# A prefix log-sum-exp scan: seven of eight batches in a hardware loop, four tile buffers instead of five

## The chip, the cores and the metric

One core of a Trainium2 chip. The metric is the device time of one execution in microseconds (us). The kernel before: 1257.1 us, median of 3 runs (1256.9 to 1266.4). All runs used below were classed as fast.

## The reference

```python
B, S, D = 8, 4096, 2048
x = np.random.randn(B, S, D).astype(np.float32)

out[:, 0, :] = x[:, 0, :]
for t in range(1, S):
    mx = np.maximum(out[:, t-1, :], x[:, t, :])
    out[:, t, :] = mx + np.log(np.exp(out[:, t-1, :] - mx) + np.exp(x[:, t, :] - mx))
```

It is a running log-sum-exp along S. Batches are independent of each other. 268 MB are read and 268 MB written, so the kernel has 537 MB to move.

## The kernel before

A batch is cut into 8 tiles of 512 rows (128 partitions x 4 rows), each 4 MB, and each tile into 4 column pieces of 512. For a piece, ScalarE takes Exp, TensorE sums down the 128 partitions with a triangular matrix, VectorE adds up the 4 rows of each partition, and ScalarE takes Ln and writes the result over the input in the same tile buffer. SyncE (SP) issues the loads, ScalarE's queue (ACTq) the stores. All 64 tiles are unrolled in the program.

```python
iopool = ctx.enter_context(tc.tile_pool(name="iopool", bufs=5))      # tile buffers
...
x_v = x.rearrange("b (k p r) d -> b k p r d", p=P, r=R)
o_v = out.rearrange("b (k p r) d -> b k p r d", p=P, r=R)
tiles = [(b, k) for b in range(B) for k in range(NBLK)]              # 8 x 8
pieces = [(b, k, c) for b, k in tiles for c in range(NC)]            # x 4

def load(b, k):
    t = iopool.tile([P, R, D], f32, name=f"io_{b}_{k}", tag="io")
    io[b, k] = t
    nc.sync.dma_start(out=t, in_=x_v[b, k])                          # L72
...
def front(b, k, c):                                                  # load, Exp, matmuls, adds
    if c == 0:
        load(b, k)
    ...
    nc.scalar.activation(et, t[:, :, cols(c)], ACT.Exp)              # L84
    ...
def back(b, k, c):
    t = io[b, k]
    nc.scalar.activation(t[:, :, cols(c)], sums.pop((b, k, c)), ACT.Ln)   # L106
    if (b, k) == tiles[-1]:
        ...                                                          # the very last tile goes out in 3 pieces
    elif c == NC - 1:
        nc.scalar.dma_start(out=o_v[b, k], in_=t)                    # L113

for n, piece in enumerate(pieces):
    front(*piece)
    if n >= 1:
        carry(*pieces[n - 1])
    if n >= LAG:                                                     # LAG = 2
        back(*pieces[n - LAG])
for piece in pieces[-LAG:]:
    back(*piece)
```

A buffer is free again when its store has landed; only then may the next load into it be issued.

The softmax here doesn't subtract the row's maximum and nothing guards it: scores larger than these inputs give would overflow.

Of the kernel before, what the change touches and what calls it, by code (L numbers as in the profile page):

```python
# [1 line left out]

# [4 lines left out]


@with_exitstack
def kernel(  # L10
    ctx: ExitStack,
    tc: tile.TileContext,
    x: bass.AP,
    out: bass.AP,
):









    nc = tc.nc
    f32 = mybir.dt.float32
    bf16 = mybir.dt.bfloat16
    ACT = mybir.ActivationFunctionType
    nc.scalar.preload_act_table_set("natural_log_exp_and_others")  # L29

    B, S, D = x.shape
    P = 128
    R = 4
    NBLK = S // (P * R)
    FD = 512
    NC = D // FD
    LAG = 2

    const = ctx.enter_context(tc.tile_pool(name="const", bufs=1))
    Li = const.tile([P, P], bf16)  # L40
    masks.make_upper_triangular(nc, Li, val=1.0, diag=True)
    Ls = const.tile([P, P], bf16)
    masks.make_upper_triangular(nc, Ls, val=1.0, diag=False)

    last = const.tile([P, P], f32)
    nc.gpsimd.memset(last, 1.0)  # L46
    nc.gpsimd.affine_select(  # L47
        out=last, in_=last, compare_op=mybir.AluOpType.is_ge, fill=0.0,
        base=-(P - 1), pattern=[[0, P]], channel_multiplier=1,
    )  # L50

    iopool = ctx.enter_context(tc.tile_pool(name="iopool", bufs=5))
    epool = ctx.enter_context(tc.tile_pool(name="epool", bufs=4))
    spool = ctx.enter_context(tc.tile_pool(name="spool", bufs=3))
    ppool = ctx.enter_context(tc.tile_pool(name="ppool", bufs=2, space=bass.MemoryType.PSUM))

    x_v = x.rearrange("b (k p r) d -> b k p r d", p=P, r=R)
    o_v = out.rearrange("b (k p r) d -> b k p r d", p=P, r=R)

    tiles = [(b, k) for b in range(B) for k in range(NBLK)]  # L60
    pieces = [(b, k, c) for b, k in tiles for c in range(NC)]
    io = {}
    sums = {}
    banks = {}

    def cols(c):
        return slice(c * FD, (c + 1) * FD)

    def load(b, k):
        t = iopool.tile([P, R, D], f32, name=f"io_{b}_{k}", tag="io")  # L70
        io[b, k] = t
        nc.sync.dma_start(out=t, in_=x_v[b, k])  # L72

    def bank(b, k, c):
        if (b, k, c) not in banks:
            banks[b, k, c] = ppool.tile([P, FD], f32, name=f"ps_{b}_{k}_{c}", tag=f"ps{c}")
        return banks[b, k, c]

    def front(b, k, c):
        if c == 0:  # L80
            load(b, k)
        t = io[b, k]
        et = epool.tile([P, R, FD], bf16, name="et")
        nc.scalar.activation(et, t[:, :, cols(c)], ACT.Exp)  # L84
        ps = bank(b, k, c)
        for r in range(R):
            nc.tensor.matmul(  # L87
                ps, Li if r == 0 else Ls, et[:, r, :],
                start=(k == 0 and r == 0), stop=(r == R - 1), skip_group_check=True,
            )  # L90
        st = spool.tile([P, R, FD], f32, name="st")
        nc.vector.tensor_copy(st[:, 0, :], ps)  # L92
        for r in range(1, R):
            nc.vector.tensor_add(st[:, r, :], st[:, r - 1, :], et[:, r, :])  # L94
        sums[b, k, c] = st

    def carry(b, k, c):
        if k < NBLK - 1:
            nc.tensor.matmul(  # L99
                bank(b, k + 1, c), last, sums[b, k, c][:, R - 1, :],  # L100
                start=True, stop=False, skip_group_check=True,
            )

    def back(b, k, c):
        t = io[b, k]
        nc.scalar.activation(t[:, :, cols(c)], sums.pop((b, k, c)), ACT.Ln)  # L106
        if (b, k) == tiles[-1]:

            if c > 0:
                part = slice(0 if c == 1 else c * FD, (c + 1) * FD)  # L110
                nc.scalar.dma_start(out=o_v[b, k][:, :, part], in_=t[:, :, part])
        elif c == NC - 1:
            nc.scalar.dma_start(out=o_v[b, k], in_=t)  # L113

    for n, piece in enumerate(pieces):
        front(*piece)
        if n >= 1:
            carry(*pieces[n - 1])
        if n >= LAG:
            back(*pieces[n - LAG])  # L120
    for piece in pieces[-LAG:]:
        back(*piece)


# [1 line left out]
_INS = ['x']  # L126
_OUTS = [((8, 4096, 2048), 'float32')]


# [23 lines left out]
```

## Time and profile before

| | |
|---|---|
| time, median | 1257.1 us |
| DMA rate in the steady part | 431 to 435 GB/s |
| DMA time of a tile, 4 MB in and 4 MB out | 19.4 us |
| ScalarE work of a tile, 8 x 1.9 us | 15.2 us |
| load, issue to landing | 31.4 us |
| store, issue to landing | 38.5 us |

From the page of the kernel before: the span, the busy time of the engines, and the two rows of DMA in 40 equal slices of the span (busy share in tenths, then GB/s).

```profile
span 1255.4 us, 5457 instructions
...
PE 636.7 (51%) x1443; PEld 216.8 (17%) x1472; DVE 703.3 (56%) x1024; ACT 930.0 (74%) x513; POOL 1.5 (0%) x10
...
DMA  9999999999999999999999999999999999999997
GB/s 401 429 430 431 435 429 433 434 433 434 434 432 433 434 432 432 433 431 432 431 431 433 434 432 434 433 434 435 431 434 431 432 432 433 432 431 431 434 428 285
```

The DMA row is full but for the last slice; no compute engine is above 74%. The Trainium skill, "DMA: Bandwidth & Descriptors", section "Where 436 GB/s comes from", gives 435 GB/s as the ceiling of the fabric (beside about 358 as HBM's share for one core, which this trace passes with one core at work), and this trace agrees: 431 to 435. Both queues always hold work, as the times to landing in the list of DMA issues show (KB of one transfer, then median us): one transfer would need about 9.7 us alone (an estimate: 4.19 MB at 432 GB/s), and takes 31 to 39 since others share the engines with it.

```profile
io<-in_x_dram SPq DMA_DIRECT2D x64, 4096.0 KB, 31.4
out_dram<-io ACTq DMA_DIRECT2D x63, 4096.0 KB, 38.5
```

The two groups of ScalarE (count, busy us, mean ns | idle us before them, and what ended most of it) and ScalarE's timeline over two tiles (start us, duration us, what, idle before and what ended it):

```profile
L84 ACT ACTIVATE et<-io 128x2048 bf16<-128x2048 f32 x256 | 485.2, 1897 | 305.8 <-DMA io<-in_x_dram 305.8
...
L106 ACT ACTIVATE io<-st 128x2048 f32<-128x2048 f32 x256 | 484.6, 1894 | 4.6 <-DVE st L94 4.5
```

```profile
615.87 1.91 ACT L84 ACTIVATE et<-io 128x2048 bf16<-128x2048 f32 x1 [4.87 <-DMA io<-in_x_dram]
...
623.21 0.34 ACTq L113 DMA_DIRECT2D out_dram<-io  x1
...
635.21 1.91 ACT L84 ACTIVATE et<-io 128x2048 bf16<-128x2048 f32 x1 [4.83 <-DMA io<-in_x_dram]
...
642.55 0.34 ACTq L113 DMA_DIRECT2D out_dram<-io  x1
```

ScalarE idles almost for one thing alone, the arrival of a load (305.8 us before Exp, L84). Its stores (L113) leave every 19.4 us, as soon as the tile's last Ln is done.

### The profile page before, as it was taken

Reading aid. Unit: us, or ns where it says so; the run is one execution under the profiler, and the core shown is the slowest. Engines: PE = TensorE matmul, PEld = TensorE weight load, DVE = VectorE, ACT = ScalarE, POOL = GpSimd, SP = SyncE. Lnnn points to the kernel's source line nnn. Section 1 sums busy time; section 2 is a strip of 40 time slices with the busy share of each in tenths; the row PEclk is TensorE's granted clock in tenths of the full one; section 3 lists DMA queues with packets and bytes.
Section 4 is the critical chain, followed back from the end, with each engine's and each line's share of the span. In section 5 each row is a group of like instructions: output and inputs, shape, how many; then the busy total and the mean of one; then the engine's idle time right before and its main releaser. Section 6 shows DMA issues by size and latency. Waiting matters only on the chain.

```text
span 1255.4 us, 5457 instructions
## 1 busy us (share of the span) xinstructions
PE 636.7 (51%) x1443; PEld 216.8 (17%) x1472; DVE 703.3 (56%) x1024; ACT 930.0 (74%) x513; POOL 1.5 (0%) x10
## 2 busy tenths in 40 slices
PE   3655445554455455554546544455455454555532
PEld 1211112111111111111111111111111121111210
DVE  3675556555565655655555556465565555655553
ACT  5987768677686786876867768677686776867865
POOL 0000000000000000000000000000000000000000
PEclk9898688785887857878577886887767878678785
DMA  9999999999999999999999999999999999999997
GB/s 401 429 430 431 435 429 433 434 433 434 434 432 433 434 432 432 433 431 432 431 431 433 434 432 434 433 434 435 431 434 431 432 432 433 432 431 431 434 428 285
DMA packets 19903, 537.22 MB, mean 428 GB/s; under 512 B 2080, under 2 KB 2080, under 8 KB 3616
## 3 DMA queue, kind: packets, MB, share of 16 engines
q1 hardware_dynamic: 9216, 268.44, 49.7%
q10 hardware_dynamic: 10656, 268.44, 49.7%
q8 instruction: 11, 0.18, 0.1%
q14 instruction: 20, 0.16, 0.0%
HBM read 268.44 MB, written 268.44 MB: 428 GB/s over the span
## 4 chain that ended last, share of the span: by engine, by line
DMA 69%; ACT 14%; DVE 5%; PE 5%; issue 5%; ACTq 0%; another core or an unknown queue 0%; DVEq 0%; SPq 0%
DMA io<-in_x_dram 67%; ACT io L106 9%; ACT et L84 5%; DVE st L94 4%; PE ps L87 3%; DMA out_dram<-io 2%; PE ps L99 2%; DVE st L92 1%; ACTq L106 0%; DVEq L94 0%; ACTq L113 0%; ACTq L84 0%; DVEq L92 0%; SPq L72 0%
## 5 line engine op out<-in xcount | busy, mean ns | idle before, releaser
L84 ACT ACTIVATE et<-io 128x2048 bf16<-128x2048 f32 x256 | 485.2, 1897 | 305.8 <-DMA io<-in_x_dram 305.8
L94 DVE TENSOR_TENSOR st<-st,et 128x512 f32<-128x512 f32 x768 | 531.0, 692 | 43.4
L106 ACT ACTIVATE io<-st 128x2048 f32<-128x2048 f32 x256 | 484.6, 1894 | 4.6 <-DVE st L94 4.5
L92 DVE COPY st<-ps 128x512 f32<-128x512 f32 x256 | 176.7, 690 | 492.5 <-PE ps L87 468.4
L99 PE MATMUL ps<-st,last 128*128 128x512 f32 x448 | 306.3, 772 | 137.6 <-DVE st L94 135.8
L87 PE MATMUL ps<-et,Li 128*128 128x512 bf16 x256 | 125.3, 489 | 459.9 <-ACT et L84 458.2
L87 PE MATMUL ps<-et,Ls 128*128 128x512 bf16 x739 | 280.5, 500 | 1.6 <-issue 1.1
L87 PEld LDWEIGHTS <-Ls 128*128 128x128 bf16 x768 | 89.5, 116 | 691.2 <-issue 662.0
L99 PEld LDWEIGHTS ps<-st,last 128*128 128x128 f32 x448 | 96.6, 238 | 249.3 <-DVE st L94 226.0
L87 PEld LDWEIGHTS <-Li 128*128 128x128 bf16 x256 | 30.7, 120 | 78.0 <-issue 70.5
L29 ACT ACT_TABLE_LOAD x1 | 1.3, 1283 | 0.8 <-PEq L137 0.8
masks.py:66 POOL TENSOR_SCALAR_AFFINE_SELECT Ls<-Ls 128x128 bf16<-128x128 bf16 x1 | 0.3, 297 | 0.0
masks.py:66 POOL TENSOR_SCALAR_AFFINE_SELECT Li<-Li 128x128 bf16<-128x128 bf16 x1 | 0.3, 296 | 0.0
L47 POOL TENSOR_SCALAR_AFFINE_SELECT last<-last 128x128 f32<-128x128 f32 x1 | 0.3, 294 | 0.1
L46 POOL MEMSET last<- 128x128 f32 x1 | 0.2, 208 | 0.0
masks.py:65 POOL MEMSET Ls<- 128x128 bf16 x1 | 0.2, 206 | 0.0
masks.py:65 POOL MEMSET Li<- 128x128 bf16 x1 | 0.2, 205 | 0.3 <-POOLq L137 0.3
L137 POOL MEMSET const-bfloat16-1.0<- 128x1 bf16 x1 | 0.1, 102 | 0.0
L137 POOL MEMSET const-uint8-127<- 128x1 uint8 x1 | 0.1, 102 | 0.0
L137 POOL MEMSET const-float32-0.0<- 128x1 f32 x1 | 0.1, 99 | 0.3 <-issue 0.3
L137 POOL MEMSET const-float32-1.0<- 128x1 f32 x1 | 0.1, 99 | 0.0
## 6 DMA issues: line engine op xcount, KB each, us to landing
io<-in_x_dram SPq DMA_DIRECT2D x64, 4096.0 KB, 31.4
out_dram<-io ACTq DMA_DIRECT2D x63, 4096.0 KB, 38.5
out_dram<-io ACTq DMA_DIRECT2D x1, 2048.0 KB, 13.2
out_dram<-io ACTq DMA_DIRECT2D x2, 1024.0 KB, 13.6
```

The lines of the kernel that those rows point to most:

```text
L29: nc.scalar.preload_act_table_set("natural_log_exp_and_others")
L46: nc.gpsimd.memset(last, 1.0)
L47: nc.gpsimd.affine_select(out=last, in_=last, compare_op=mybir.AluOpType.is_ge, fill=0.0, base=-(P - 1), pattern=[[0, P]], channel_multipl ...
L84: nc.scalar.activation(et, t[:, :, cols(c)], ACT.Exp)
L87: nc.tensor.matmul(ps, Li if r == 0 else Ls, et[:, r, :], start=(k == 0 and r == 0), stop=(r == R - 1), skip_group_check=True,)
L92: nc.vector.tensor_copy(st[:, 0, :], ps)
L94: nc.vector.tensor_add(st[:, r, :], st[:, r - 1, :], et[:, r, :])
L99: nc.tensor.matmul(bank(b, k + 1, c), last, sums[b, k, c][:, R - 1, :], start=True, stop=False, skip_group_check=True,)
L106: nc.scalar.activation(t[:, :, cols(c)], sums.pop((b, k, c)), ACT.Ln)
L137: nc = _bacc.Bacc("TRN2", target_bir_lowering=False, num_devices=1)
```

## The change

The intent is a program of an eighth of the size: the body of one batch is traced once, and run seven times by a hardware loop without a barrier between iterations; the eighth batch stays unrolled, because its last tile goes out in pieces. An iteration has 8 tiles, so the buffers go from 5 to 4, which divides 8 and lets every iteration use them in the same order.

```diff
-    iopool = ctx.enter_context(tc.tile_pool(name="iopool", bufs=5))
+    iopool = ctx.enter_context(tc.tile_pool(name="iopool", bufs=4))
...
-    tiles = [(b, k) for b in range(B) for k in range(NBLK)]
-    pieces = [(b, k, c) for b, k in tiles for c in range(NC)]
...
+    def batch(b, final):
+        pieces = [(k, c) for k in range(NBLK) for c in range(NC)]
+        xb = x_v[b] if isinstance(b, int) else x_v[bass.ds(b, 1)][0]
+        ob = o_v[b] if isinstance(b, int) else o_v[bass.ds(b, 1)][0]
...      # front, carry and back as before, with (k, c) for (b, k, c)
-        nc.sync.dma_start(out=t, in_=x_v[b, k])
+                nc.sync.dma_start(out=io[k], in_=xb[k])              # L78
...
-            nc.scalar.dma_start(out=o_v[b, k], in_=t)
+                nc.scalar.dma_start(out=ob[k], in_=io[k])            # L108
...
+    with tc.For_i(0, B - 1, 1, iteration_sync="reg_based") as b:
+        batch(b, False)
+    batch(B - 1, True)
```

More of the change, by code (lines that the diff above doesn't have):

```diff
@@ L58 @@
     o_v = out.rearrange("b (k p r) d -> b k p r d", p=P, r=R)
-    tiles = [(b, k) for b in range(B) for k in range(NBLK)]
-    pieces = [(b, k, c) for b, k in tiles for c in range(NC)]
-    io = {}
-    sums = {}
-    banks = {}
     def cols(c):
         return slice(c * FD, (c + 1) * FD)
-    def load(b, k):
-        t = iopool.tile([P, R, D], f32, name=f"io_{b}_{k}", tag="io")
-        io[b, k] = t
-        nc.sync.dma_start(out=t, in_=x_v[b, k])
-    def bank(b, k, c):
-        if (b, k, c) not in banks:
-            banks[b, k, c] = ppool.tile([P, FD], f32, name=f"ps_{b}_{k}_{c}", tag=f"ps{c}")
-        return banks[b, k, c]
@@ L79, in front @@
-    def front(b, k, c):
-        if c == 0:
-            load(b, k)
-        t = io[b, k]
-        et = epool.tile([P, R, FD], bf16, name="et")
-        nc.scalar.activation(et, t[:, :, cols(c)], ACT.Exp)
-        ps = bank(b, k, c)
-        for r in range(R):
-            nc.tensor.matmul(
-                ps, Li if r == 0 else Ls, et[:, r, :],
-                start=(k == 0 and r == 0), stop=(r == R - 1), skip_group_check=True,
-            )
-        st = spool.tile([P, R, FD], f32, name="st")
-        nc.vector.tensor_copy(st[:, 0, :], ps)
-        for r in range(1, R):
-            nc.vector.tensor_add(st[:, r, :], st[:, r - 1, :], et[:, r, :])
-        sums[b, k, c] = st
@@ L97, in carry @@
-    def carry(b, k, c):
-        if k < NBLK - 1:
-            nc.tensor.matmul(
-                bank(b, k + 1, c), last, sums[b, k, c][:, R - 1, :],
-                start=True, stop=False, skip_group_check=True,
-            )
-    def back(b, k, c):
-        t = io[b, k]
-        nc.scalar.activation(t[:, :, cols(c)], sums.pop((b, k, c)), ACT.Ln)
-        if (b, k) == tiles[-1]:
-            if c > 0:
-                part = slice(0 if c == 1 else c * FD, (c + 1) * FD)
-                nc.scalar.dma_start(out=o_v[b, k][:, :, part], in_=t[:, :, part])
-        elif c == NC - 1:
-            nc.scalar.dma_start(out=o_v[b, k], in_=t)
@@ L115, with bank, front, carry @@
-    for n, piece in enumerate(pieces):
-        front(*piece)
-        if n >= 1:
-            carry(*pieces[n - 1])
-        if n >= LAG:
-            back(*pieces[n - LAG])
-    for piece in pieces[-LAG:]:
-        back(*piece)
+    def batch(b, final):
+        pieces = [(k, c) for k in range(NBLK) for c in range(NC)]
+        io, sums, banks = {}, {}, {}
+        xb = x_v[b] if isinstance(b, int) else x_v[bass.ds(b, 1)][0]
+        ob = o_v[b] if isinstance(b, int) else o_v[bass.ds(b, 1)][0]
+        def bank(k, c):
+            if (k, c) not in banks:
+                banks[k, c] = ppool.tile([P, FD], f32, name=f"ps{k}_{c}", tag=f"ps{c}")
+            return banks[k, c]
+        def front(k, c):
+            if c == 0:
+                io[k] = iopool.tile([P, R, D], f32, name=f"io{k}", tag="io")
+                nc.sync.dma_start(out=io[k], in_=xb[k])
+            et = epool.tile([P, R, FD], bf16, name="et")
+            nc.scalar.activation(et, io[k][:, :, cols(c)], ACT.Exp)
+            ps = bank(k, c)
+            for r in range(R):
+                nc.tensor.matmul(
+                    ps, Li if r == 0 else Ls, et[:, r, :],
+                    start=(k == 0 and r == 0), stop=(r == R - 1), skip_group_check=True,
+                )
+            st = spool.tile([P, R, FD], f32, name="st")
+            nc.vector.tensor_copy(st[:, 0, :], ps)
+            for r in range(1, R):
+                nc.vector.tensor_add(st[:, r, :], st[:, r - 1, :], et[:, r, :])
+            sums[k, c] = st
+        def carry(k, c):
+            if k < NBLK - 1:
+                nc.tensor.matmul(
+                    bank(k + 1, c), last, sums[k, c][:, R - 1, :],
+                    start=True, stop=False, skip_group_check=True,
+                )
+        def back(k, c):
+            nc.scalar.activation(io[k][:, :, cols(c)], sums.pop((k, c)), ACT.Ln)
+            if final and k == NBLK - 1:
+                if c > 0:
+                    part = slice(0 if c == 1 else c * FD, (c + 1) * FD)
+                    nc.scalar.dma_start(out=ob[k][:, :, part], in_=io[k][:, :, part])
+            elif c == NC - 1:
+                nc.scalar.dma_start(out=ob[k], in_=io[k])
+        for n, piece in enumerate(pieces):
+            front(*piece)
+            if n >= 1:
+                carry(*pieces[n - 1])
+            if n >= LAG:
+                back(*pieces[n - LAG])
+        for piece in pieces[-LAG:]:
+            back(*piece)
```

## The prediction

> **What bounds the kernel now.** The 16 DMA engines. The page's slices show DMA at 9 tenths in all but the last, at 431 to 435 GB/s; 537 MB moved at 432 GB/s is 1243 us of the 1255 us span. The Trainium skill, "DMA: Bandwidth & Descriptors", section "Where 436 GB/s comes from", puts the ceiling at 435 GB/s; this trace agrees. ScalarE is busy 74%; the chain that ended last is 67% loads. One 4 MB tile in plus 4 MB out is 19.4 us of DMA time; ScalarE needs 15.2 us per tile (8 x 1.9) and idles about 5 us waiting for the load.
>
> A smaller term: the landing records of each transfer's 16 parts show one engine falling behind the fastest, from 0.6 us to about 11 us at the end, in steps of about 0.9 us at instruction-fetch packets. The slowest engine ends every transfer, so fetches cost up to 10 us.
>
> **What the change does.**
> 1. Four buffers for five. A buffer's cycle is load 31.4 us + compute 26.7 us (load landed to store issued: 615.9 to 642.55 in the timeline) + store 38.9 us = 97 us = 5 x 19.4. With four it must be 77.6 us, leaving 50.9 us for load and store together: they need at least 19.4, two or three buffers are always in the queues, so the engines stay fed. Latencies fall to about 25 us each; cost about 0 to 2 us.
> 2. Back edges, 7. No barrier; store and load issue wait on buffers across iterations. An iteration's last two Ln come before the next one's first Exp; ScalarE idles a little, inside its slack. About 0.
> 3. Instruction supply. Register waits lengthen the body, and a back edge may refetch it. The Trainium skill, "Runtime: NRT & Kernel Launch", section "Instruction fetch mechanics", says that a taken branch whose target isn't in the two-page window forces a fetch; no trace here shows a branch yet. If the body stays resident, the lag of the slowest engine vanishes (-10 us); if it is refetched each iteration, the lag grows (up to +15). Mean 0.
> 4. Entry and exit. I expect the loop to own its semaphores, to be entered after a meeting of the engines (+3 us), and left by waiting for all of its work and clearing them: the DMA pipeline drains once, before the eighth batch. Worked out from the end of this trace: the last load lands at 1221.5, the last store at 1254.4: 33 us, with about 20 us of DMA work in them, so 10 to 13 us idle, plus about 3 us to restart. +13 to 16 us, on the critical path. I give this drain 80%.
>
> Loads, stores and compute stay the same.
>
> **Predicted time.** 1257 + 14 (exit, weighted) + 3 (entry) - 2 (supply, buffers) = 1272 us; 8 in 10 in 1250 to 1294. Faster by over 2%: 0.01 (the floor is about 1243). Within 2%: 0.73. Slower: 0.26.
>
> **What would show it.** Step 1: DMA slices at 9 tenths and about 432 GB/s in the loop; load and store to landing about 25 us. Step 2: no dips every 155 us. Step 3: packets on the instruction queues, and the spread of the 16 landings. Step 4: one or two low slices near 7/8 of the span (about 1100 us), with loads restarting after the last store.
>
> **What would make it wrong.** If the first load of an iteration waits for all stores of the previous one, each edge drains: +15 us x 7, about 1370. If the exit doesn't drain and code stays resident, about 1247. If four buffers leave the queues empty for part of each tile, GB/s falls everywhere and the time grows in proportion.

## The result, and the profile after

1439.1 us, median of 4 runs (1438.3 to 1441.0), against 1257.1 us. The ratio is 1.143, with a 95% interval of 1.138 to 1.148. Ratios here and below are the mean time of one kernel's fast runs over the mean of the other's fast runs of the same rounds, so not quite the ratio of the medians quoted. The result is outside the predicted 1250 to 1294 us.

The same lines of the page after:

```profile
span 1438.3 us, 7702 instructions
...
PE 630.8 (44%) x1447; PEld 209.0 (15%) x1472; DVE 696.5 (48%) x1024; ACT 932.4 (65%) x513; POOL 1.5 (0%) x10
...
DMA  9989889899898989989898998988989899799997
GB/s 392 381 346 392 356 362 382 350 394 365 365 379 350 394 365 379 365 350 394 362 392 354 365 380 365 394 350 365 379 365 394 350 379 365 336 383 428 425 429 319
```

The busy times of PE, DVE and ACT have moved by 1% or less. The rate has fallen to about 370 GB/s, alike in all seven looped batches, and is 425 to 429 in the unrolled eighth. There are no deep dips every 180 us, so it is not a pipeline that drains at each back edge. The busy tenths hardly show the loss (8 and 9 for 9); the row of GB/s does.

```profile
io<-in_x_dram SPq DMA_DIRECT2D x64, 4096.0 KB, 22.4
out_dram<-io ACTq DMA_DIRECT2D x63, 4096.0 KB, 22.6
```

Times to landing are shorter than before, and almost equal to each other. The groups and the timeline of ScalarE say why:

```profile
L101 ACT ACTIVATE io<-st 128x2048 f32<-128x2048 f32 x256 | 485.1, 1898 | 360.1 <-DMA out_dram<-io 324.9
L80 ACT ACTIVATE et<-io 128x2048 bf16<-128x2048 f32 x256 | 482.5, 1894 | 132.3 <-issue 75.7
```

```profile
224.94 1.89 ACT L101 ACTIVATE io<-st 128x2048 f32<-128x2048 f32 x1
226.74 1.89 ACT L80 ACTIVATE et<-io 128x2048 bf16<-128x2048 f32 x1
236.37 0.36 ACTq L108 DMA_DIRECT2D out_dram<-io  x1
236.84 1.91 ACT L101 ACTIVATE io<-st 128x2048 f32<-128x2048 f32 x1 [8.20 <-DMA out_dram<-io]
...
249.46 1.89 ACT L80 ACTIVATE et<-io 128x2048 bf16<-128x2048 f32 x1
259.35 0.36 ACTq L108 DMA_DIRECT2D out_dram<-io  x1
259.82 1.91 ACT L101 ACTIVATE io<-st 128x2048 f32<-128x2048 f32 x1 [8.47 <-DMA out_dram<-io]
```

Before, ScalarE waited for loads (305.8 us). Now it waits 324.9 us for the landing of a *store*. (The 75.7 us before Exp that the page puts down to "issue" are the same wait at the six back edges: each comes just after a late store.) The last Ln ahead of the store ends at 226.83 us, and the store of 236.37 leaves 9.5 us later. ScalarE has slack, so its own pause is not what lengthens the tile: its work for the next store is done before 252 us, and that store leaves only at 259.35. The trace's landing records (first and last of the 16 parts of a transfer, us from the span's start) say what it waited for:

```
store landed 235.7 to 236.2      load landed 235.5 to 236.1
issued at 236.37: a store; at 236.36: a load
store landed 258.5 to 259.2      load landed 258.3 to 259.1
issued at 259.35: the next store
```

So one load and one store are in flight at a time. They start together, share the DMA engines, land together, and then for a moment nothing is in flight. Stretches of the trace, split at those moments (from:to, length, busy us of PE, PEld, DVE, ACT, POOL with instructions, granted TensorE clock, DMA share, GB/s); first after, then before:

```profile
238.00:257.50 19.50, 11.97 (x24) 3.74 (x24) 11.08 (x16) 13.35 (x8) 0.00 (x0) 0.68 0.94 403
257.50:260.00 2.50, 0.10 (x1) 0.00 (x0) 0.00 (x0) 0.18 (x1) 0.00 (x0) 0.50 0.04 13
260.00:280.20 20.20, 11.24 (x23) 3.74 (x24) 10.99 (x16) 14.33 (x8) 0.00 (x0) 0.69 1.02 415
280.20:282.70 2.50, 0.00 (x0) 0.00 (x0) 0.00 (x0) 0.24 (x1) 0.00 (x0) 1.00 0.01 0
```

```profile
603.80:623.20 19.40, 6.53 (x17) 2.29 (x17) 11.07 (x16) 14.53 (x9) 0.00 (x0) 0.58 1.00 432
```

A tile takes 20.2 + 2.5 = 22.7 us where it took 19.4. Over the iterations two to six the packet records have 41 moments of over 0.2 us with no packet in flight, 1.6 us each on average (40 tiles pass in that time); the same stretch of the kernel before has none.

The landing records also share out the whole difference. Every 16th transfer to land is about the end of a batch (us):

```
                end of batch    1      2      3      4      5      6      7      8     last
before                        166.8  322.6  479.4  635.1  791.9  947.7 1104.4 1249.3  1254.4
after                         190.6  371.9  553.0  734.1  915.0 1095.8 1270.3 1429.8  1435.2
longer in after, per batch    +23.8  +25.5  +24.3  +25.4  +24.1  +25.0  +17.8  +14.6   +0.3
```

Of 181 us, 148 are the steady 3.1 us per tile of batches one to six; batch seven and eight, with the drain at the loop's exit between them, make up 32.

Why does a store wait for the one before? The compiled programs list what each store's issue waits for, and the traces record the same waits. Three neighbouring stores of each (names of the DMA semaphores; "own" is cut):

```
before   store n     waits  DMAHW1, Activation       after   store n     waits  DMAHW3, Activation
         store n+1   waits  DMAHW3, Activation               store n+1   waits  DMAHW6, Activation
         store n+2   waits  DMAHW5, Activation               store n+2   waits  DMAHW0, Activation
```

They look alike, and are not. Before, stores raise the semaphores 1, 3, 5, 7 in turn, and each waits for the last use of its own one, four stores back, which has long landed. After, the semaphore named is the one that the store just before it raises. The traces record, for each issue, the semaphores that it waits for and the one that it raises: in the changed kernel 55 of the 56 looped stores (all but the first) wait for the semaphore of the store just before, in the kernel before none does. The stores of an iteration write to different rows, so nothing in the data asks for this order.

**Theory A.** The loop's register in the stores' address makes the compiler order each store behind the landing of the one before. With loads released by landing stores, load and store fall into step, and each tile pays one round of landing, issue and restart with idle DMA engines. **Theory B:** four buffers are too few. **Theory C:** the loop's extra instructions and back edges slow the engines (7702 instructions for 5457). **Theory D:** the order of the stores hurts only together with four buffers.

### The profile page after: what moved, and what is told of

It reads as the page before. It is cut to its first block, busy times and chain, and to the rows that moved or that the text cites. A ratio compares the mean times of both kernels' runs of the same rounds, so it can differ in the third digit from the quotient of the medians.

```text
span 1438.3 us, 7702 instructions
## 1 busy us (share of the span) xinstructions
PE 630.8 (44%) x1447; PEld 209.0 (15%) x1472; DVE 696.5 (48%) x1024; ACT 932.4 (65%) x513; POOL 1.5 (0%) x10
## 5 line engine op out<-in xcount | busy, mean ns | idle before, releaser
L101 ACT ACTIVATE io<-st 128x2048 f32<-128x2048 f32 x256 | 485.1, 1898 | 360.1 <-DMA out_dram<-io 324.9
L80 ACT ACTIVATE et<-io 128x2048 bf16<-128x2048 f32 x256 | 482.5, 1894 | 132.3 <-issue 75.7
L95 PE MATMUL ps<-st,last 128*128 128x512 f32 x448 | 293.3, 742 | 158.6 <-DVE st L90 157.9
L95 PEld LDWEIGHTS ps<-st,last 128*128 128x128 f32 x448 | 87.9, 220 | 272.0 <-DVE st L90 231.3
## 6 DMA issues: line engine op xcount, KB each, us to landing
out_dram<-io ACTq DMA_DIRECT2D x63, 4096.0 KB, 22.6
```

Source lines behind the costliest of these rows:

```text
L80: nc.scalar.activation(et, io[k][:, :, cols(c)], ACT.Exp)
L95: nc.tensor.matmul(bank(k + 1, c), last, sums[k, c][:, R - 1, :], start=True, stop=False, skip_group_check=True,)
L101: nc.scalar.activation(io[k][:, :, cols(c)], sums.pop((k, c)), ACT.Ln)
```

## The experiments

All results were correct unless said otherwise. "before" stood at 1257.0 to 1257.2 us (medians) in each group of runs.

### e1: the loop, with the stores' order declared away

```diff
+    def free(s):
+        tc.add_to_no_dep_group("stores", s.ins)
+        tc.declare_no_dep(s.ins, group="stores", across_iterations=True, reason="stores go to different rows of out")
...
-                nc.scalar.dma_start(out=ob[k], in_=io[k])
+                s = nc.scalar.dma_start(out=ob[k], in_=io[k])
+                if not final:
+                    free(s)
```

The rows are disjoint, so this stays free of races.

> The changed kernel, with the order between the loop's stores declared unnecessary: no store waits for the one before it any more; loop, register waits, four buffers and the drain at the exit stay. Theory A (each store waits until the store before it has landed, load and store then start and end together, and about 3.3 us per tile pass with no transfer: 22.7 us per tile where 19.4 would do): 1252 to 1275 us, DMA slices back at 9 tenths in the loop, one dip near 7/8 for the exit. Theory B (four buffers are too few): about 1439. Theory C (register waits, register arithmetic and back edges slow the engines): about 1439, or above 1350.

Measured: 1278.1 us (1274.7 to 1280.6), ratio 1.016 (1.014 to 1.018). That is 161 us of the 182 back, with loop, register waits and four buffers all in place. In its trace no store waits for the one before. Theories B and C fall; the time is 3 us above what A allowed. The DMA rows of its page, and what ScalarE's Exp waited for (total us, times, longest):

```profile
DMA  9999999999999999999999999999999997899997
GB/s 381 425 437 431 430 441 427 430 441 427 432 439 427 434 437 430 435 435 429 437 430 422 420 431 422 431 429 427 429 426 423 423 431 324 345 426 411 441 429 318
```

```profile
ACT et L84 <- DMA io<-in_x_dram: 298.6, 53, 25.4
```

The loop runs at the old rate, ScalarE waits for loads again, and what is left to see is one dip in the slices of 324 and 345 GB/s: the drain at the loop's exit, where the loop's work is waited for before the eighth batch starts.

### e2 and e9: four buffers, no loop

```diff
-    iopool = ctx.enter_context(tc.tile_pool(name="iopool", bufs=5))
+    iopool = ctx.enter_context(tc.tile_pool(name="iopool", bufs=4))
```

> The kernel before with four tile buffers where there are five, nothing else. Theory A: 1250 to 1265 us, loads and stores landing about 25 us after issue, DMA at 430 GB/s. Theory B: near 1439. Theory C: 1257.

Measured: 1264.4 us (1260.0 to 1273.9), ratio 1.008 (1.003 to 1.013). Theory B falls a second time. As the interval was wide, the same kernel ran again with more rounds:

> The kernel of e2 again (unrolled, four buffers), with five rounds, because e2's interval of 0.3 to 1.3 per cent is too wide to share out 21 us. If four buffers cost 7 us: 1262 to 1266 us. If e2 was high by chance: 1257 to 1261.

Measured: 1268.7 us (1267.2 to 1275.1), ratio 1.010 (1.008 to 1.012), above both expected ranges. Four buffers cost about 1%: 12 us here (10 to 15 by the interval), 7 in e2, and 11 in e6 below, which orders its stores besides. Loads land after 27.1 us and stores after 24.4, as the arithmetic of the prediction had it (about 25 each), and in batches two to six no moment without packets is found. The loss shows as a slightly lower rate late in the run. The same stretch in e9 and before:

```profile
792.00:948.00 156.00, 76.49 (x178) 26.05 (x180) 86.50 (x127) 113.70 (x64) 0.00 (x0) 0.77 1.00 423
```

```profile
792.00:948.00 156.00, 77.31 (x180) 26.59 (x184) 88.10 (x128) 116.28 (x65) 0.00 (x0) 0.77 1.00 433
```

Both have a DMA share of 1.00, and 423 against 433 GB/s. Why packets take longer there is not shown.

### e3: the order of the stores alone, no loop, four buffers

To e2's kernel is added:

```diff
-            nc.scalar.dma_start(out=o_v[b, k], in_=t)
+            s = nc.scalar.dma_start(out=o_v[b, k], in_=t)
+            if stores:
+                tc.add_manual_dep(s.ins, stores[-1].name,
+                    mybir.DependencyInfo(mybir.DependencyClass.Sync, mybir.DependencyReason.DATA),
+                    reason="one store at a time")
+            stores.append(s.ins)
```

> The kernel before with four buffers, and each store made to wait for the landing of the store before it; no loop. Theory A: about 22.7 us per tile for all 64 tiles, so 1440 to 1475 us. Theories B and C differ: B 1439 (and the four-buffer run alone shows it already), C about 1257.

Measured: 1472.8 us (1471.3 to 1473.2), ratio 1.171 (1.169 to 1.173): the slowdown without any loop, in all eight batches. Its page and its list of DMA issues look like those of the changed kernel:

```profile
span 1471.5 us, 5461 instructions
...
GB/s 399 397 331 369 377 338 396 355 347 371 356 389 342 370 383 342 385 354 359 357 356 385 356 371 385 342 379 349 371 377 336 385 356 371 360 351 386 350 378 342
...
io<-in_x_dram SPq DMA_DIRECT2D x64, 4096.0 KB, 22.6
out_dram<-io ACTq DMA_DIRECT2D x63, 4096.0 KB, 22.7
```

### e4: the changed kernel with five buffers

```diff
-    iopool = ctx.enter_context(tc.tile_pool(name="iopool", bufs=4))
+    iopool = ctx.enter_context(tc.tile_pool(name="iopool", bufs=5))
```

> The changed kernel with five buffers again; the loop's stores still wait for one another. Theory A: a fifth buffer can't help for long, because each load is released by a landing store and the backlog of loads is used up in the gaps: 1410 to 1445 us. Theory B: 1257 to 1280. Theory D (the chain of stores hurts only together with four buffers): 1257 to 1290. Theory C: about 1439.

Measured: 1382.1 us (1378.7 to 1386.8), ratio 1.100 (1.097 to 1.103). This is between A and B or D, and a miss for all of them. The stores do wait on each other (55 of 56, as in the changed kernel). But an iteration of 8 tiles starts again with the first of 5 buffers, and so the loads do not keep step with the stores: once per batch three loads leave within 1.2 us (199.61 to 200.75), other stores run with no load beside them, and the packet records have 5 moments without packets per batch where the changed kernel has 8. The rate swings between about 345 and 435 GB/s within a batch. The run mixes two things, so e5 asks the question without the loop.

### e5: the order of the stores alone, five buffers

The edit of e3 on the kernel before, five buffers kept.

> The kernel before, with its five buffers, and each store made to wait for the landing of the store before it. Run e4 (loop, five buffers) gave 1382, below what theory A said, but there the loop restarts its buffers in the same order each iteration, which mixes two things. Here nothing but the chain is added. Theory A (load and store fall into step whatever the number of buffers): 1440 to 1475 us. Theory D (a fifth buffer keeps a load queued during the gap between stores): 1257 to 1300. Between them: the fifth buffer delays the falling into step or softens it.

Measured: 1469.7 us (1467.8 to 1470.3), ratio 1.169 (1.167 to 1.171). Theory D falls: with five buffers the order of the stores costs what it costs with four. A fifth buffer gives the loads one tile of lead, and yet from 81.69 us on each load leaves within 0.05 us of a store. That the gaps use the lead up is argued, not shown. The packet records of this run have 40 moments without packets between 190 and 1096 us, 1.6 us each, as e3 (39) and the changed kernel (41).

### e6: two stores in flight

e3's kernel, with each store behind the store two before it:

```diff
-            if stores:
-                tc.add_manual_dep(s.ins, stores[-1].name, ...
+            if len(stores) >= 2:
+                tc.add_manual_dep(s.ins, stores[-2].name, ...
```

> As e3 (unrolled, four buffers), but each store waits for the store two before it, so that two may be in flight. Theory A: the next store is queued before the last one lands, no gap: 1257 to 1275 us, as e2. If the waiting itself costs (an instruction that waits on ScalarE's in-order queue), a good part of the 200 us of e3 stays: above 1350.

Measured: 1267.8 us (1265.4 to 1269.0), ratio 1.008 (1.007 to 1.010), as e9 without any order, and no moment without packets until 1241 us, at its end. Waiting on a store is not what costs; having no second store queued when one lands is.

### e8: the loop, with a fixed address for the stores

```diff
-        ob = o_v[b] if isinstance(b, int) else o_v[bass.ds(b, 1)][0]
+        ob = o_v[b] if isinstance(b, int) else o_v[0]
```

> The changed kernel with one edit: inside the loop the stores go to batch 0's rows by a fixed address instead of the address made from the loop's register (a wrong result on purpose: batches 1 to 6 are never written). No order is declared away. If the register in the address is what makes each store wait for the one before: the waits are gone and the time is e1's, 1265 to 1285 us. If the loop as such orders its stores: about 1439.

Measured: 1279.6 us (1275.2 to 1283.3), ratio 1.019 (1.015 to 1.022); the result is wrong, on purpose. With the register out of the stores' address, and nothing declared away, the waits between an iteration's stores are gone from the compiled program and from the trace (none of the 56), and the time is e1's. Fixing the *loads'* address instead was compiled but not run; the waits between stores stayed. It is the register in the written address that brings them. Writing the address with the tile's index first and the register after it was compiled too, and changed nothing.

### e7 and e10: all eight batches in the loop

e1, with all eight batches in the loop, so that there is no exit before the eighth:

```diff
-    with tc.For_i(0, B - 1, 1, iteration_sync="reg_based") as b:
+    with tc.For_i(0, B, 1, iteration_sync="reg_based") as b:
         batch(b, False)
-    batch(B - 1, True)
```

> As e1, but all eight batches run in the loop, so that nothing is drained between the seventh and the eighth; the last tile is stored whole. If e1's 21 us over the kernel before are 7 us of four buffers and 14 us of the drain at the exit: 1260 to 1267 us. If the loop, which fetched no code in its later iterations, also saves what code fetches cost the kernel before: 1245 to 1257.

Measured: 1272.8 us (1270.9 to 1275.6), ratio 1.012 (1.010 to 1.014). That is outside both ranges: by the medians 5 us under e1 and 4 above e9. After the first iteration this kernel fetches no code, yet is no faster than the unrolled one with as many buffers. Its end differs too, since its last tile goes out whole. e10 was to take that away, by storing the last tile of every batch in three pieces:

```diff
-            if final and k == NBLK - 1:
+            if k == NBLK - 1:
                 if c > 0:
                     part = slice(0 if c == 1 else c * FD, (c + 1) * FD)
-                    nc.scalar.dma_start(out=ob[k][:, :, part], in_=io[k][:, :, part])
+                    free(nc.scalar.dma_start(out=ob[k][:, :, part], in_=io[k][:, :, part]))
```

> As e7 (all eight batches in the loop, no store waits for another), but the last tile of each batch is stored in three pieces, as the kernel before stores its very last tile. This takes away the longer tail of e7, so that what is left against e1 is the drain at the exit alone. If e7 lost about 5 us to its whole last store: 1265 to 1270 us, and the drain at the exit cost e1 about 10 us. If the drain costs 14: 1264. If the pieces themselves cost per batch: 1273 or more.

Measured: 1302.7 us (1301.4 to 1303.3), ratio 1.036 (1.035 to 1.037). This is the third of the expected cases: the pieces cost about 30 us over eight batches (against e7), so the run says nothing of the exit. Its rate falls to 348 to 371 GB/s once per batch. Two things are seen there, and the run does not part them: 14,592 packets under 8 KB where e7 has 2,048, and one moment of 2.6 us without packets per batch.

### e11: e1 with five buffers

> As e1 (loop of seven, no store waits for another), with five buffers. If four buffers cost e1 some 7 us: 1268 to 1273 us. If the restart of the five buffers in the same order each iteration costs as much as the fifth buffer gives: 1278, as e1, or more.

Measured: 1277.9 us (1275.1 to 1281.1), ratio 1.016 (1.014 to 1.017), the same as e1. In this loop the fifth buffer returns nothing.

No run beat the kernel before; the best with a loop, e7, is 1.2% slower.

## Why the prediction was wrong

The step that failed is the one that said of the loop's transfers "store and load issue wait on buffers across iterations", at a cost of "About 0", and "Loads, stores and compute stay the same." The loads did wait on buffers. The stores waited on each other: the address with the loop's register made the compiler put each store behind the landing of the store before. In place of about 0 this cost some 161 us (the changed kernel against e1: 1439.1 - 1278.1), 2.9 us for each of the 56 looped tiles. e1 and e8 take the waits away and the cost goes; e3 and e5 add them to the unrolled kernel and it comes; e6 shows that it is the lack of a second store in flight. The prediction looked for barriers and drains at the edges of iterations, and for its own alternative of a drain per edge it named 1370 us; the cost was inside the iteration, once per tile. Its last alternative named the symptom, queues that are empty for part of each tile, but blamed the four buffers, which cost 12 us alone (e9). With the waits gone the same loop took 1278 us, 6 us from the 1272 predicted and inside its range; that it came so close is partly luck, since the buffers cost more than predicted and exit and entry less (below).

Point by point:

- *DMA is the limit.* Right for the kernel before: its packet records have no moment of over 0.2 us without packets, and ScalarE, the busiest compute engine, has 930 to 932 us of work in every run. In the changed kernel the DMA engines are no longer kept full, 1.6 us of each tile.
- *Four buffers cost 0 to 2 us.* The mechanism was right (loads and stores landed after 27.1 and 24.4 us, no moment without packets), the size was not: e9 gives 12 us (10 to 15).
- *No cost at back edges.* Right for barriers: in the changed kernel stores leave 22.8 us apart across an edge (190.88 and 213.68 us), about as within an iteration (22.6, from 168.28 to 190.88), and e1 has no dip every 155 us.
- *Code supply, mean 0.* No run sizes the net by itself. The body stayed resident: between 99 and 1257 us of the changed kernel no instruction packet is recorded. But the 10 us that the prediction expected from that did not come (e7 is 4 us slower than e9). In the kernel before, the lag of the slowest DMA engine does grow by 0.9 to 1.0 us at fetches, as the prediction said (from 2.3 to 3.3 us at the one of 258.3 us, for example). But in e7, with no fetch between 94 and 1271 us, the slowest engine still fell about 10 us behind the fastest. So taking the fetches away does not take the lag away; what makes it in the loop is open.
- *The exit drains the pipeline, 13 to 16 us, and the entry costs 3.* The drain is there (the slices of 324 and 345 GB/s in e1), and the first load left at 2.25 us instead of 0.81. Together e1 over e9 is 0.6% by the ratios, 8 us (9 by the medians), where the prediction's two terms came to 17: about twice too large, if nothing else differs between e1 and e9. e7 and e10 could not size the exit by itself.

What stays open: why four buffers lower the rate by a few GB/s at a full DMA share; what makes one DMA engine lag; and how the 21 us of e1 divide between exit and buffers to better than a few us.

## What to carry to other kernels

When a loop's register goes into the address of a store, look at what each store of the compiled program waits for before trusting that independent rows stay independent; on a kernel bound by DMA a needless wait for the store just before can leave the DMA engines idle, here 3 us in every 23. Keep a second transfer queued in each direction when one lands (e6 was enough), since a load that is released by a landing store starts in step with the next store, and a fifth buffer alone did not break the step (e5). Read the GB/s row, not the busy tenths: here 9s and 8s hid a loss of 14%.

## What the Trainium skill lacked or had wrong

- "DMA: Bandwidth & Descriptors" lists what the fixed cost of a DMA is made of (for the software path), but not what it costs two streams that release each other: with one load and one store in flight, and the next of both issued on landing, no packet was in flight for 1.6 us, and almost nothing moved for 2.5 us in every 22.7 (0.01 to 0.04 of the DMA share).
- The same page, section "Latency and other measured facts", gives about 0.6 us to the first byte for such DMAs. In the changed kernel the first packet after a gap started about 0.9 us after the issue of a store began, of which the issue itself took 0.36: in agreement, if the page counts from the end of the issue, which it doesn't say.
- "Runtime: NRT & Kernel Launch", section "Instruction fetch mechanics", says that a branch out of the two-page window forces a fetch, and doesn't say what a loop that fits pays: here no instruction packet is recorded between 99 and 1257 us, in the second to the seventh iteration of 181 us.
- "DMA: Bandwidth & Descriptors", section "Latency and other measured facts", says that DMA engines 7 and 15 are usually slower, and gives software descriptor rings as a best guess for it. Here all data went through the hardware queues, and the slowest of the 16 engines still fell 10 us behind, by 1104 us in the kernel before and by 640 us in e7. The records don't name it, so whether it is one of those two is not shown.
